# RWKV state chain moved one unit later, its steps interleaved with the next units' matmul groups

## The chip, the core and the metric

One core of one Trainium2 chip runs the whole program. The metric is the device time of one execution in microseconds (us), lower being better. Executions of this kernel are compared by the median of several runs; traces come from one profiled execution.

## What is computed

One decoder layer over a sequence of 1024 tokens of width 1024, in float32. A combined projection feeds three token mixers (RWKV-7, latent attention called MLA, differential attention), their outputs are gated, summed and projected, and a convolutional feed-forward network follows. The change is in the RWKV-7 mixer. It has 8 heads of 64 channels, each with a 64x64 state that every token updates:

```python
def step(state, inp):
    r_t, w_t, k_t, v_t, kk_t, b_t = inp
    sa = jnp.einsum('bhij,bhj->bhi', state, -kk_t)
    state = (state * w_t[:, :, None, :] + sa[..., None] * b_t[:, :, None, :]
             + v_t[..., None] * k_t[:, :, None, :])
    return state, jnp.einsum('bhij,bhj->bhi', state, r_t)
```

The outputs are then normalised per head (`ln_w`, `ln_b`), a bonus term `(sum r*k*r_k) * v` is added, and the result is multiplied by a gate.

## The kernel before, in words

**Units and chunks.** RWKV is cut into 8 units: four pairs of heads `p`, each in two halves `f` of 512 tokens. A unit holds 8 chunks `c` of 64 tokens; the two heads of a pair lie on partitions 0 to 63 and 64 to 127. The work inside a chunk is turned into matrix products, so that only one small matrix recurrence is left from chunk to chunk, the chain of states.

**The three parts of a unit.** `rw_front` (L465) makes the decays and keys: two low-rank products (tile `lps`, two passes each), a norm (`pss`, `prx`), the bonus (`pbo`, L532 to L537), two groups `pA` of products within the chunks, a group of transposes `ptb`, and, by two trips through DRAM (`zf`, `ze`) and 30 short VectorE instructions (`zt`, `zd`, L568), the inverses of 16x16 blocks. `rw_back` (L588) has nine groups of small matmuls, `ptv`, `ph`, `pe`, `ph`, `pe`, `pk`, `pg`, `pq`, `pw`, `pyc`, which leave `ft`, `fc`, `qt`, `yc`. `rw_chain` (L673) runs the chain: for each chunk, two 64x64 matmuls `pr` (L694), and one VectorE instruction that makes the next state `st` (L695); then the group `py`, and the normalisation, two groups of transposes `pty`, the gate product `lpg`, and a store to DRAM (L728). Each of these matmuls is float32 and shows as two passes in the trace, so a chain step is `pr` x4.

**The loop.** `rwkv` (L347) goes over the 8 units: front of unit n, the projections of the next pair in every second iteration (`project`, L350), then back and chain of unit n-1. After the loop come back and chain of the last unit.

**What sets the order.** The program is traced in this order and a scheduler reorders it: each engine takes, of the instructions that its model of the time says are ready, the one with the highest priority, which is the order of tracing; `later` (L366) lowers the priority of projections by 500000, of fills by a million. `keep_in_program_order` pins an instruction behind the one traced before it on its engine. Between fixed points the scheduler is free.

**Fills.** 40 blocks of the combined projection that RWKV doesn't need (tile `gps`, 48 matmuls of 128x512 each, `fills` L385, evicted to `sp` and stored to `pD`) are cover for the waits of RWKV. `nfill` (L67) says how many are traced after each iteration: 3, then 4 seven times, then 3 and 3, 37 in all; the last three are traced after RWKV (L1734). `fill` (L373) paces them: 60% (`share`) of an iteration's fill matmuls are spread evenly over the `mark`s that RWKV set in that iteration, from the fourth mark on (`skip` 3), each not to be issued before its mark; the other 40% come after the last mark. The three last ones have one mark, the last of RWKV. Marks stand before nearly every group of `rw_back` and before each chain step.

**Buffers.** Tiles from `T1` have one buffer: among them `ft`, `fc`, `qt`, `yc`, `kp`, `st`. PSUM has one buffer for each of the tags `ms`, `ab`, `ch`, `y`. Weight loads of fills and projections share two buffers `raw`.

**After RWKV.** `mla_open` (L1234) loads what the MLA mixer needs (`craw`, L931) into memory that RWKV's tiles held and makes keys `kps` and queries `qps`; the attention proper (`S`, `vps`) begins when the last fills are done.

Of the kernel before, what the change touches and what calls it, by code (L numbers as in the profile page):

```python
# [61 lines left out]
class Emit:  # L62
# [6 lines left out]
    def __init__(self, tc, i, o):  # L69
        self.tc, self.nc, self.i, self.o = tc, tc.nc, i, o  # L70
        self.pace, self.marks, self.marking, self.paced = None, [], False, False
        self.pinned = self.strict = False


    def mm(self, out, lhsT, rhs, start=True, stop=True, **k):
        ins = self.nc.tensor.matmul(out, lhsT, rhs, start=start, stop=stop, **k)  # L76
        if self.pinned:
            self.tc.keep_in_program_order(ins)
        if self.pace is not None:
            marks, total, done = self.pace  # L80
            m = len(marks)
            at = lambda d: min(m - 1, int(d * m / total))
            if done == 0 or at(done) != at(done - 1):
                self.tc.add_manual_dep(ins.ins, marks[at(done)], mybir.DependencyInfo(
                    mybir.DependencyClass.NoSync, mybir.DependencyReason.DATA), reason="issue order")
            self.pace[2] += 1
        self.marked(ins)

    def tr(self, out, in_, ident):
        ins = self.nc.tensor.transpose(out, in_, ident)  # L90
        if self.pinned:
            self.tc.keep_in_program_order(ins)
        self.marked(ins)

# [200 lines left out]
    def rwkv(self, rc, r1, r2, zp, pp):  # L295
# [48 lines left out]
        units = [(p, f) for p in range(4) for f in range(2)]  # L344
        state, prev = None, None
# [118 lines left out]

    def rw_front(self, par, p, f, rt, kt, vt):  # L465

# [7 lines left out]

        ps = lora(self.lw[0], self.lx[0], A, p, f)
        th = T1("th")
        self.act(th, ps, AF.Tanh, scale=0.5, bias=self.hw0[:, p:p + 1])
        self.ts(th, th, 1.0, 1.0, ALU.mult, ALU.add, pool)
        cs = T1("cs")
# [19 lines left out]

        ps = lora(self.lw[0], self.lx[0], B, p, f)  # L500
        ta = T1("ta")
        self.act(ta, ps, AF.Tanh, scale=0.5, bias=self.ha0[:, p:p + 1])
        kp = T1("kp")
# [26 lines left out]
        self.tt(bk[:, :, 1], c3(kp), bk[:, :, 1], ALU.mult, pool)  # L530

        self.stt(kp, rt, self.v("rk", p), kp, ALU.mult, ALU.mult)  # L532
        pm = pp.tile([128, 512], F32, tag="ms", name="pbo")
        self.mm(pm, self.bones, kp)
        bv = u["bv"] = T2("bv")
        self.tt(bv, pm, vt, ALU.mult)
        self.ts(bv, bv, 1.0, self.v("lnb", p), ALU.mult, ALU.add, pool)  # L537


        am = u["am"] = T2("am", (128, 2, 8, 3, 64))  # L540
        for q in range(2):
            self.mark()
            pA = pp.tile([128, 2, 4, 2, 64], F32, tag="ab", name="pA")
            for c in range(4):
                for h, hs in half:
                    self.mm(pA[:, h, c].rearrange("p s t -> p (s t)"),
                            bk[hs, 4 * q + c, h:h + 2].rearrange("p s t -> p (s t)"),
                            ar[hs, 4 * q + c, 2:4].rearrange("p s t -> p (s t)"))
            for h, hs in half:
                self.tt(am[:, h, 4 * q:4 * q + 4, 0:2].rearrange("p c s t -> p c (s t)"),  # L550
# [26 lines left out]
        u["ze"] = self.ze[par]  # L577
        return u

# [7 lines left out]

    def rw_back(self, u):  # L588

# [10 lines left out]
        sv = T1("sv", (128, 3, 8, 64))  # L600
        self.mark()
        pt = pp.tile([128, 2, 8, 64], F32, tag="ab", name="ptv")
# [6 lines left out]
        for l in range(2):  # L609
            ml = T1("ml", (128, 8, 64))  # L610
            for h, hs in half:
                self.tt(ml[hs], am[hs, h, :, 0], self.lvl[hs, l].unsqueeze(1).to_broadcast([64, 8, 64]), ALU.mult, pool)
            self.mark()
# [11 lines left out]
            if l == 1:  # L625
                em = T1("ml", (128, 8, 64))
# [7 lines left out]
        self.mark()  # L634
        pk = pp.tile([128, 8, 64], F32, tag="ms", name="pk")
        for c in range(8):
            for h, rs, os in ((0, B, A), (1, A, B)):
                self.mm(pk[os, c], am[rs, h, c, 0], sv[rs, h, c])
        self.act(sv[:, 2], pk)
        self.mark()  # L640
        pg = pp.tile([128, 8, 2, 64], F32, tag="ab", name="pg")
        for c in range(8):
            for h, hs in half:
                self.mm(pg[hs, c], em[hs, c], sv[hs, h:3:2 - h, c])
        gt = T1("hm", (128, 8, 64))
        self.act(gt, pg[:, :, 0])
        for h, hs in half:
            vec.tensor_copy(sv[hs, h], pg[hs, :, 1])
        self.mark()
        pq = pp.tile([128, 8, 2, 64], F32, tag="ab", name="pq")  # L650
        for c in range(8):
            for h, hs in half:
                self.mm(pq[hs, c], gt[hs, c], am[hs, h, c, 1:3])
        qt = u["qt"] = T1("qt", (128, 8, 64))
# [3 lines left out]
        self.mark()  # L658
        pw = pp.tile([128, 8, 64], F32, tag="ms", name="pw")
        for c in range(8):  # L660
            for h, hs in half:
                self.mm(pw[hs, c], am[:, h, c, 2], sv[:, h, c])
        fc = u["fc"] = T1("fc", (128, 8, 64))
        self.tt(fc, pw, gam[:, 1:9].unsqueeze(2).to_broadcast([128, 8, 64]), ALU.mult)
        self.mark()
        pw = pp.tile([128, 8, 64], F32, tag="ms", name="pyc")
        for c in range(8):
            for h, hs in half:
                self.mm(pw[hs, c], am[:, h, c, 1], sv[:, h, c])
        yc = u["yc"] = T1("yc", (128, 8, 64))  # L670
        self.act(yc, pw)

    def rw_chain(self, u, state):  # L673
        nc = self.nc
# [4 lines left out]
        c3 = lambda t: t.rearrange("p (c t) -> p c t", c=8)  # L679
        p, f, gam = u["p"], u["f"], u["gam"]  # L680
        ft, fc, qt = u["ft"], u["fc"], u["qt"]
        st = T1("st", (128, 9, 64))
        if f == 0:
            pool.memset(st[:, 0], 0.0)
        else:
            self.ts(st[:, 0], state, gam[:, 0:1])
        for c in range(8):
            if f == 0 and c == 0:
                vec.tensor_copy(st[:, 1], fc[:, 0])
                continue  # L690
            self.mark()
            pr = pp.tile([128, 64], F32, tag="ch", name="pr")
            for h, hs in half:
                self.mm(pr[hs], ft[hs, c], st[hs, c])  # L694
            self.stt(st[:, c + 1], pr, gam[:, c + 1:c + 2], fc[:, c], ALU.mult, ALU.add)  # L695
        end = T2("end", (128, 64))
        vec.tensor_copy(end, st[:, 8])
        self.mark()
        py = pp.tile([128, 8, 64], F32, tag="y", name="py")
        for c in range(8):  # L700
            for h, hs in half:
                self.mm(py[hs, c], qt[hs, c], st[hs, c])

        y = u["yc"]
        self.tt(y, py, y, ALU.add)
        m8 = T1("m8", (128, 8))
# [21 lines left out]
        nc.sync.dma_start(self.oD[0, p, :, 512 * f:512 * f + 512], ot)  # L728
        return end

# [1113 lines left out]
```

## Time and profile before

| | |
|---|---|
| runs shown, median (lowest to highest) | 2108.87 us (2105.81 to 2109.48), 3 runs |
| the profiled execution | 2112.69 us |
| its span in the trace | 2110.9 us |
| TensorE (PE) busy, weight loads (PEld) busy | 96%, 77% |
| VectorE (DVE), ScalarE (ACT), GpSimd (POOL) busy | 55%, 39%, 34% |

The span is the time from the first to the last instruction of the program; the execution's time has 1.8 us around it. RWKV and its fills take the stretch from about 97 to 893 us. In the rows a matmul's `busy` time includes the drain of the pipeline, so consecutive matmuls overlap in the trace; what a matmul costs is read from start to start. "issue" as the end of an idle time means that the engine waited for nothing that the profile shows.

### The profile page before, as it was taken

What the parts mean: (1) busy time and instruction counts of PE and PEld (TensorE: products, weight loads), DVE (VectorE), ACT (ScalarE), POOL (GpSimd) and SP (SyncE); (2) the same over time, 40 slices, a digit from 0 to 9 for tenths busy, and PEclk for the clock granted to TensorE, in tenths of its full rate; (3) what the DMA queues carried; (4) which work ended last, traced back from release to release, by engine and by line L of the source; (5) the groups of instructions that cost most, each with busy time, mean ns of one, the idle gap of its engine ahead of it and who ended that gap; (6) DMA issues with size and microseconds to landing.
All of it is one profiled execution on the core that took longest, in us unless ns stands there. A gap on an engine that the chain in (4) does not pass through costs nothing. (4 is left out here: it accounts for less than half of the span.)

```text
span 2110.9 us, 32553 instructions
## 1 busy us (share of the span) xinstructions
PE 2034.2 (96%) x12554; PEld 1625.7 (77%) x12554; DVE 1154.0 (55%) x2273; ACT 826.4 (39%) x1449; POOL 709.8 (34%) x577
## 2 busy tenths in 40 slices
PE   7999999999999999999989898999999999999998
PEld 6877777777777777777768776787788888888887
DVE  7135254343534532476777786457866677653534
ACT  5332322232222221577555553234544444442332
POOL 3143243243333322446143656313534433400000
PEclk9999999999999999999989999999999999999999
DMA  5213122212213223320066645353222222264641
GB/s 183 87 62 91 56 73 66 75 66 79 80 46 94 65 66 104 105 65 11 16 211 185 178 135 192 111 181 111 90 90 91 74 77 90 80 238 146 228 141 66
DMA packets 141565, 221.83 MB, mean 105 GB/s; under 512 B 61632, under 2 KB 65600, under 8 KB 141408
## 3 DMA queue, kind: packets, MB, share of 16 engines
q1 hardware_dynamic: 141264, 219.21, 32.0%
q8 instruction: 99, 1.62, 0.3%
q14 instruction: 58, 0.48, 0.1%
q10 hardware_dynamic: 144, 0.52, 0.1%
HBM read 162.53 MB, written 57.16 MB: 104 GB/s over the span
## 5 line engine op out<-in xcount | busy, mean ns | idle before, releaser
L76 PE MATMUL gps<-hhi,whi 128*128 128x512 f32 (+1 forms) x880 | 345.6, 396 | 8.4 <-ACT sp L102 5.9
L76 PE MATMUL gps<-hlo,whi 128*128 128x512 f32 (+1 forms) x880 | 341.6, 391 | 0.0
L109 POOL TENSOR_TENSOR wlo<-wraw,whi 128x512 fp32r<-128x512 f32 x130 | 169.9, 1317 | 297.6 <-PE gps L76 148.7
L76 PE MATMUL gps<-hhi,wlo 128*128 128x512 f32 (+1 forms) x880 | 226.1, 393 | 2.1 <-DVE lx L119 1.7
L76 PEld LDWEIGHTS gps<-hhi,whi 128*128 128x128 f32 x880 | 167.2, 190 | 49.7 <-ACT sp L102 7.5
L76 PEld LDWEIGHTS gps<-hlo,whi 128*128 128x128 f32 x880 | 167.2, 190 | 35.9 <-issue 3.7
L76 PEld LDWEIGHTS gps<-hhi,wlo 128*128 128x128 f32 x880 | 157.4, 188 | 43.1 <-issue 6.8
L109 POOL TENSOR_TENSOR rs_r<-rs_v,phalf 128x1 f32<-128x1 f32 (+2 forms) x43 | 40.5, 942 | 386.0 <-DVE rs_v L116 376.6
L102 ACT ACTIVATE whi<-wraw 128x512 fp32r<-128x512 f32 x130 | 81.4, 628 | 188.0 <-DMA wraw<-in_w_rest_dram 107.2
L102 ACT ACTIVATE L<-L,m 128x128 f32<-128x128 f32 (+7 forms) x128 | 98.9, 773 | 67.6 <-DVE m L109 46.6
L102 ACT ACTIVATE wh<-wsum 128x512 fp32r<-128x512 f32 x109 | 68.5, 630 | 129.5 <-PE ups_b L76 56.0
L109 POOL TENSOR_TENSOR wl<-wraw,wh 128x512 fp32r<-128x512 f32 x43 | 58.3, 1358 | 150.9 <-PE ups_c L76 109.8
L109 DVE TENSOR_TENSOR wsum<-wraw 128x512 f32<-128x512 f32 x110 | 82.0, 749 | 40.6 <-POOL wl L109 39.4
L119 DVE SCALAR_TENSOR_TENSOR st<-pr,gam,fc 128x64 f32<-128x64 f32 x60 | 17.0, 283 | 128.0 <-PE pr L76 127.8
L109 DVE TENSOR_TENSOR gl<-graw,gh 128x512 fp32r<-128x512 f32 x42 | 28.9, 691 | 105.1 <-ACT gh L102 105.1
L90 PE MATMUL ptp<-ident,L 128*128 128x128 f32 x432 | 72.2, 282 | 9.8 <-DVE L L119 2.6
L109 POOL TENSOR_TENSOR wl<-wsum,wh 128x512 fp32r<-128x512 f32 x43 | 57.4, 1336 | 72.0 <-PE ups_b L76 53.8
L102 ACT ACTIVATE gh<-graw 128x512 fp32r<-128x512 f32 x42 | 26.4, 632 | 128.7 <-PE dps__20229 L76 63.6
L90 PEld LDWEIGHTS ptp<-ident,L 128*128 128x128 f32 x432 | 48.9, 141 | 26.3 <-issue 15.0
L902 DVE CUSTOM_DVE_ANT_0 L<-S,mband,rq 128x512 f32<-128x512 f32 (+3 forms) x96 | 57.2, 612 | 18.1 <-PE S L76 9.0
L102 ACT ACTIVATE cvp<-C,cw 128x1024 f32<-128x1024 f32 x44 | 53.1, 1207 | 29.4 <-DVE C L109 19.0
L102 ACT ACTIVATE sp<-gps,hbg 128x512 f32<-128x512 f32 x48 | 33.0, 687 | 75.3 <-PE gps L76 69.8
(769 smaller groups left out, 5119.6 us busy)
## 6 DMA issues: line engine op xcount, KB each, us to landing
wraw<-in_w_up_dram SPq DMA_DIRECT2D x44, 512.0 KB, 4.3
wdr<-in_w_down_dram SPq DMA_DIRECT2D x42, 512.0 KB, 3.4
wraw<-in_w_rest_dram SPq DMA_DIRECT2D x80, 256.0 KB, 2.9
pD<-sp SPq DMA_DIRECT2D x78, 256.0 KB, 2.0
gth<-pD SPq DMA_DIRECT2D x48, 256.0 KB, 2.9
gD<-cv SPq DMA_DIRECT2D x21, 512.0 KB, 2.6
graw<-gD SPq DMA_DIRECT2D x42, 256.0 KB, 2.6
x<-in_x_dram SPq DMA_DIRECT2D x16, 512.0 KB, 6.1
```

What stands on the lines that cost most here:

```text
L76: ins = self.nc.tensor.matmul(out, lhsT, rhs, start=start, stop=stop, **k)
L90: ins = self.nc.tensor.transpose(out, in_, ident)
L102: return self.kept(self.nc.scalar.activation(out, in_, func, **kw))
L109: self.kept((eng or self.nc.vector).tensor_tensor(out, a, b, op))
L119: return self.kept(self.nc.vector.scalar_tensor_tensor(out, a, s, b, op0, op1))
L902: self.nc.vector.tensor_tensor_reduce(L[:, c0:c0 + w], ps[:, :w], bias[:, c0:c0 + w], scale, 3.0e38, ALU.add, ALU.min, acc)
```

## The change

The chain of unit n-2 is now traced during the front of unit n and the back of unit n-1. `chain_steps` is a generator; `step()` takes its next step, right after a group has been traced (both `pA`, `ptb`, first `ph`, `pe` with `pk`, second `ph`, second `pe`, `pg`). `next_on_pe` pins the first matmul that follows it behind the instruction traced before it on TensorE. The same is done for the second low-rank product (`lpa`, right behind `lps`), for `pk` behind `pe`, and for `pw` and `pyc` behind `pq`. What follows the chain is `chain_out`, after the back; the bonus comes after it. Only the last unit's chain is alone (`alone=True`), with marks as before. Chain steps and the pinned groups set no mark otherwise, so that an iteration with front and back has 12 marks. The loop has a ninth iteration without a front, and its fill: 40 fills are traced within RWKV.

```diff
     def mm(self, out, lhsT, rhs, start=True, stop=True, **k):
         ins = self.nc.tensor.matmul(out, lhsT, rhs, start=start, stop=stop, **k)
-        if self.pinned:
+        if self.pinned or self.follow:
             self.tc.keep_in_program_order(ins)
+            self.follow = False
...
-        for n, (p, f) in enumerate(units):
-            u = self.rw_front(n % 2, p, f, *[raw.pop((nm, p, f)) for nm in "rkv"])
+        for n, (p, f) in enumerate(units + [(None, None)]):
+            steps = self.chain_steps(last, state) if last else iter(())
+            step = lambda: next(steps, None)
+            if p is not None:
+                u, bonus = self.rw_front(n % 2, p, f, *[raw.pop((nm, p, f)) for nm in "rkv"], step)
+            if prev:
+                self.rw_back(prev, step)
+            for _ in steps:
+                pass
+            if last:
+                state = self.chain_out(last)
+            if p is not None:
+                bonus()
             if f == 1 and p < 3:
                 with self.later(500000):
                     project(p + 1)
-            if prev:
-                self.rw_back(prev)
-                state = self.rw_chain(prev, state)
-            prev = u
+            prev, last = u, prev
             self.fill(fills, self.nfill[n + 1])
-        self.rw_back(prev)
-        self.rw_chain(prev, state)
+        for _ in self.chain_steps(last, state, True):
+            pass
+        self.chain_out(last)
         self.fill(fills, self.nfill[9])
...
+    def next_on_pe(self):
+
+        self.follow = True
...
         ps = lora(self.lw[0], self.lx[0], A, p, f)
+        self.next_on_pe()
+        psa = lora(self.lw[0], self.lx[0], B, p, f, pp.tile([128, 512], F32, tag="ms", name="lpa"))
...
+            step()
             for h, hs in half:
                 self.tt(am[:, h, 4 * q:4 * q + 4, 0:2].rearrange("p c s t -> p c (s t)"),
...
+        ml = levels(0)
+
         self.mark()
         pt = pp.tile([128, 2, 8, 64], F32, tag="ab", name="ptv")
...
+            self.next_on_pe()
+            pk = pp.tile([128, 8, 64], F32, tag="ms", name="pk")
+            for c in range(8):
+                for h, rs, os in ((0, B, A), (1, A, B)):
+                    self.mm(pk[os, c], am[rs, h, c, 0], sv[rs, h, c])
+            step()
             self.tt(de, pe, de, ALU.add)
...
+        step()
         gt = T1("hm", (128, 8, 64))
         self.act(gt, pg[:, :, 0])
         for h, hs in half:
             vec.tensor_copy(sv[hs, h], pg[hs, :, 1])
+
+        while step():
+            pass
         self.mark()
         pq = pp.tile([128, 8, 2, 64], F32, tag="ab", name="pq")
...
+        self.next_on_pe()
+        pw = pp.tile([128, 8, 64], F32, tag="ms", name="pw")
...
+        self.next_on_pe()
+        py = pp.tile([128, 8, 64], F32, tag="y", name="pyc")
...
+    def chain_steps(self, u, state, alone=False):
...
+        for c in range(1 - u["f"], 8):
+            if alone:
+                self.mark()
+            else:
+                self.next_on_pe()
+            pr = pp.tile([128, 64], F32, tag="ch", name="pr")
             for h, hs in half:
+                self.mm(pr[hs], ft[hs, c], st[hs, c])
+            self.stt(st[:, c + 1], pr, gam[:, c + 1:c + 2], fc[:, c], ALU.mult, ALU.add)
+            if c == 7:
+                self.next_on_pe()
+                py = u["py"] = pp.tile([128, 8, 64], F32, tag="y", name="py")
+                for k in range(8):
+                    for h, hs in half:
+                        self.mm(py[hs, k], qt[hs, k], st[hs, k])
+                end = u["end"] = self.T2("end", (128, 64))
+                vec.tensor_copy(end, st[:, 8])
+                y = u["y"] = st[:, 0:8]
+                self.tt(y, py, u["yc"], ALU.add)
+            yield True
```

## Rows read from the trace of the kernel before

**Rows 1.** The page: span, then busy time, share and instructions of each engine.

```profile
span 2110.9 us, 32553 instructions
PE 2034.2 (96%) x12554; PEld 1625.7 (77%) x12554; DVE 1154.0 (55%) x2273; ACT 826.4 (39%) x1449; POOL 709.8 (34%) x577
```

**Rows 2.** Windows: busy us (and instructions) by engine, granted clock, DMA share, GB/s.

```profile
97.00:615.00 518.00, 511.37 (x4001) 394.06 (x4000) 215.97 (x522) 140.19 (x242) 178.65 (x158) 0.99 0.23 68
```

**Rows 3.** Timeline of PE: start, us, engine, line, operation, tiles, count. A lone chain step.

```profile
430.60 0.39 PE L76 MATMUL gps<-hhi,whi 128*128 128x512 f32 x1
430.82 0.39 PE L76 MATMUL gps<-hlo,whi 128*128 128x512 f32 x1
431.14 0.33 PE L76 MATMUL pr<-st,ft 64*64 64x64 f32 x4
...
431.52 0.50 PE L76 MATMUL gps<-hhi,whi 128*128 128x512 f32 x1
431.86 0.39 PE L76 MATMUL gps<-hlo,whi 128*128 128x512 f32 x1
```

**Rows 4.** Timeline of PE, a chain step behind another group, and `py` alone before it.

```profile
405.65 0.33 PE L76 MATMUL py<-st,qt 64*64 64x64 f32 x4
...
405.91 1.15 PE L76 MATMUL pyc<-sv,am 128*64 128x64 f32 x32
...
406.99 0.33 PE L76 MATMUL pr<-st,ft 64*64 64x64 f32 x4
...
407.15 0.28 PE L76 MATMUL py<-st,qt 64*64 64x64 f32 x4
...
407.37 0.53 PEld L76 LDWEIGHTS gps<-hhi,wlo 128*128 128x128 f32 x3
```

**Rows 5.** Tile `pr`: what its engine waited for (us, times).

```profile
  issue: 12.3, 36
```

**Rows 6.** Groups of PE and PEld, 97 to 893 us: count | busy, mean ns | idle before.

```profile
L76 PEld LDWEIGHTS gps<-hlo,whi 128*128 128x128 f32 x767 | 145.2, 189 | 33.1 <-issue 3.7
L76 PE MATMUL pq<-am,hm 64*64 64x128 f32 x256 | 15.7, 272 | 1.9 <-DVE sv L648 1.9
L76 PEld LDWEIGHTS pr<-st,ft 64*64 64x64 f32 x240 | 12.0, 131 | 16.8 <-issue 12.3 <-DVE st L119 2.3 <-DVE sq L517 1.1
```

**Rows 7.** Timeline: the end of a unit's projections, where the weights change.

```profile
414.53 0.33 PE L76 MATMUL pr<-st,ft 64*64 64x64 f32 x4
...
415.25 0.33 PE L76 MATMUL pr<-st,ft 64*64 64x64 f32 x4 [0.27 <-DVE st L119]
...
416.38 0.47 PE L76 MATMUL gps<-hhi,whi 128*128 128x512 f32 x1 [0.69 <-DVE kt L119]
```

**Rows 8.** Groups of POOL and DVE, 97 to 893 us, columns as in rows 6.

```profile
L109 POOL TENSOR_TENSOR ml<-am,lvl 64x512 f32<-64x512 f32 x32 | 41.5, 1296 | 33.1 <-PE ph L76 18.6 <-PE pg L76 13.3
L109 DVE TENSOR_TENSOR zd<-zd,zt 64x15 f32<-64x15 f32 (+7 forms) x120 | 40.1, 334 | 3.8
L119 DVE SCALAR_TENSOR_TENSOR st<-pr,gam,fc 128x64 f32<-128x64 f32 x60 | 17.0, 283 | 128.0 <-PE pr L76 127.8
L116 POOL TENSOR_SCALAR kp<-ta,hka,cka 128x512 f32<-128x512 f32 x8 | 6.7, 836 | 2.5 <-PE pbo L76 2.4
```

**Rows 9.** Tile `ot`: the store of a unit on the SP queue (ns minimum, median, maximum).

```profile
L728 SPq DMA_DIRECT2D oD<-ot x8: 326/332/1468, 293.3 to 836.6; - x8
```

**Rows 10.** Timeline, end of RWKV to the end of the last query.

```profile
846.30 0.63 ACT L102 ACTIVATE whi<-wraw 128x512 fp32r<-128x512 f32 x1 [6.60 <-DMA wraw<-in_w_rest_dram]
...
850.59 0.80 PE L76 MATMUL gps<-hhi,whi 128*128 128x512 f32 x1 [5.09 <-ACT sp L102]
...
885.45 0.68 DVE L109 TENSOR_TENSOR qtl<-qf,qth 32x512 fp32r<-32x512 f32 x1 [0.80 <-ACT qth L102]
```

**Rows 11.** Windows after that stall, columns as in rows 2.

```profile
851.00:860.00 9.00, 9.00 (x30) 7.10 (x30) 7.23 (x8) 3.76 (x9) 2.98 (x4) 0.72 0.55 173
```

**Rows 12.** End of RWKV, window 835 to 893 us of tile `gps` (columns as rows 2, without POOL).

```profile
835.00:893.00 58.00, 46.52 (x186) 36.65 (x186) 0.00 (x0) 5.48 (x8) 0.94 0.43 129
```

More of the change, by code (lines that the diff above doesn't have):

```diff
@@ L76, in mm @@
         ins = self.nc.tensor.matmul(out, lhsT, rhs, start=start, stop=stop, **k)
-        if self.pinned:
+        if self.pinned or self.follow:
             self.tc.keep_in_program_order(ins)
+            self.follow = False
         if self.pace is not None:
@@ L90, in tr @@
         ins = self.nc.tensor.transpose(out, in_, ident)
-        if self.pinned:
+        if self.pinned or self.follow:
             self.tc.keep_in_program_order(ins)
+            self.follow = False
         self.marked(ins)
@@ L344, in rwkv @@
         units = [(p, f) for p in range(4) for f in range(2)]
-        state, prev = None, None
+        state, prev, last = None, None, None
         project(0)
-        for n, (p, f) in enumerate(units):
-            u = self.rw_front(n % 2, p, f, *[raw.pop((nm, p, f)) for nm in "rkv"])
+        for n, (p, f) in enumerate(units + [(None, None)]):
[11 more added lines that the diff above has]
+                bonus()
             if f == 1 and p < 3:
@@ L463, in lora, with rw_front @@
         return ps
-    def rw_front(self, par, p, f, rt, kt, vt):
+    def rw_front(self, par, p, f, rt, kt, vt, step):
         nc = self.nc
@@ L530, in rw_front, with bonus @@
         self.tt(bk[:, :, 1], c3(kp), bk[:, :, 1], ALU.mult, pool)
[L532 to L537, printed above, removed]
+        def bonus():
+            self.stt(kp, rt, self.v("rk", p), kp, ALU.mult, ALU.mult)
+            pm = pp.tile([128, 512], F32, tag="ms", name="pbo")
+            self.mm(pm, self.bones, kp)
+            bv = u["bv"] = T2("bv")
+            self.tt(bv, pm, vt, ALU.mult)
+            self.ts(bv, bv, 1.0, self.v("lnb", p), ALU.mult, ALU.add, pool)
         am = u["am"] = T2("am", (128, 2, 8, 3, 64))
@@ L577, in rw_front @@
         u["ze"] = self.ze[par]
-        return u
+        return u, bonus
     @staticmethod
@@ L586, in diag, with rw_back @@
         return bass.AP(t.tensor, t.offset + 66560 * m, [[1040, 64], [64, 16], [1, 16]])
-    def rw_back(self, u):
+    def rw_back(self, u, step):
         nc = self.nc
@@ L600, in rw_back, with levels @@
         sv = T1("sv", (128, 3, 8, 64))
+        def levels(l):
+            ml = T1("ml", (128, 8, 64))
+            for h, hs in half:
+                self.tt(ml[hs], am[hs, h, :, 0], self.lvl[hs, l].unsqueeze(1).to_broadcast([64, 8, 64]), ALU.mult, pool)
+            return ml
+        ml = levels(0)
         self.mark()
@@ L609, in rw_back @@
         for l in range(2):
[L610 to L613, printed above, removed]
+            if l:
+                ml = levels(1)
+                self.mark()
             ph = pp.tile([128, 8, 64], F32, tag="ms", name="ph")
@@ L625, in rw_back @@
             if l == 1:
+                step()
                 em = T1("ml", (128, 8, 64))
@@ L631, in rw_back @@
                     self.mm(pe[hs, 0, c], em[hs, c], hm[hs, c])
-            self.tt(de, pe, de, ALU.add)
[L634 to L639, printed above, removed]
+            self.next_on_pe()
[3 more added lines that the diff above has]
+                    self.mm(pk[os, c], am[rs, h, c, 0], sv[rs, h, c])
+            step()
+            self.tt(de, pe, de, ALU.add)
+            self.act(sv[:, 2], pk)
         self.mark()
@@ L644, in rw_back @@
                 self.mm(pg[hs, c], em[hs, c], sv[hs, h:3:2 - h, c])
+        step()
         gt = T1("hm", (128, 8, 64))
@@ L653, in rw_back @@
                 self.mm(pq[hs, c], gt[hs, c], am[hs, h, c, 1:3])
+        self.next_on_pe()
+        pw = pp.tile([128, 8, 64], F32, tag="ms", name="pw")
+        for c in range(8):
+            for h, hs in half:
+                self.mm(pw[hs, c], am[:, h, c, 2], sv[:, h, c])
+        self.next_on_pe()
+        py = pp.tile([128, 8, 64], F32, tag="y", name="pyc")
+        for c in range(8):
+            for h, hs in half:
+                self.mm(py[hs, c], am[:, h, c, 1], sv[:, h, c])
         qt = u["qt"] = T1("qt", (128, 8, 64))
@@ L657, in rw_back, with chain_out @@
         self.tt(ft, pq[:, :, 1], self.id64.unsqueeze(1).to_broadcast([128, 8, 64]), ALU.add)
[L658 to L662, printed above, removed]
         fc = u["fc"] = T1("fc", (128, 8, 64))
         self.tt(fc, pw, gam[:, 1:9].unsqueeze(2).to_broadcast([128, 8, 64]), ALU.mult)
-        self.mark()
-        pw = pp.tile([128, 8, 64], F32, tag="ms", name="pyc")
-        for c in range(8):
-            for h, hs in half:
[L669 to L673, printed above, removed]
+        yc = u["yc"] = T1("yc", (128, 8, 64))
+        self.act(yc, py)
+    def chain_steps(self, u, state, alone=False):
+        nc = self.nc
+        pool, vec, pp = nc.gpsimd, nc.vector, self.pp
+        half = ((0, slice(0, 64)), (1, slice(64, 128)))
+        ft, fc, qt, gam = u["ft"], u["fc"], u["qt"], u["gam"]
+        st = u["st"] = self.T1("st", (128, 9, 64))
+        if u["f"] == 0:
+            pool.memset(st[:, 0], 0.0)
+            vec.tensor_copy(st[:, 1], fc[:, 0])
+        else:
+            self.ts(st[:, 0], state, gam[:, 0:1])
+        for c in range(1 - u["f"], 8):
+            if alone:
+                self.mark()
+            else:
+                self.next_on_pe()
+            pr = pp.tile([128, 64], F32, tag="ch", name="pr")
+            for h, hs in half:
+                self.mm(pr[hs], ft[hs, c], st[hs, c])
[4 more added lines that the diff above has]
+                for k in range(8):
+                    for h, hs in half:
+                        self.mm(py[hs, k], qt[hs, k], st[hs, k])
[4 more added lines that the diff above has]
+            yield True
+    def chain_out(self, u):
         nc = self.nc
@@ L679, in rw_chain @@
         c3 = lambda t: t.rearrange("p (c t) -> p c t", c=8)
[L680 to L705, printed above, removed]
+        p, f, y = u["p"], u["f"], u["y"]
         m8 = T1("m8", (128, 8))
@@ L728, in rw_chain @@
         nc.sync.dma_start(self.oD[0, p, :, 512 * f:512 * f + 512], ot)
-        return end
+        return u["end"]
     def bias_band(self, sp, pp):
```

5 lines of the change are left out of this document (2 added, 3 removed).

## The prediction

> **What bounds the kernel now.** I read the page first: PE is busy 96% of the span, the other engines at most 55% [rows 1]. A busy share says little of a pipelined engine, so I looked at the stretch that the change touches. From 97 to 615 us PE is busy 511 of 518 us, at a granted clock of 0.99 [rows 2]. Hardly anything there waits: fills stand in every hole. So a shorter latency of the chain buys nothing by itself; PE's own sequence has to get shorter. What can get shorter is seen in the timeline. Fills follow each other by 0.22 to 0.23 us (430.60 to 430.82; 0.23 below). A lone chain step with its share of `py` takes 1.04 us from the last fill before it to the second after it, where two fill steps take 0.46: it costs **0.58** [rows 3]. The same pair behind `pyc` costs 0.38 (406.99 to 407.37) [rows 4]. The difference, 0.20, is what entering and leaving a run of small matmuls costs: the first comes 0.32 after the last fill instead of 0.23, and the first fill after the run takes 0.50 instead of 0.39 [rows 3]. The tile view of `pr` counts the entries that waited for nothing but "issue": 36 [rows 5], of 60 steps (240 loads, four a step) [rows 6].
>
> **The change, part by part.**
>
> *Steps behind groups.* 36 lone steps lose 0.20 each: 36 x 0.20 = **-7.2 us**. The steps that today join another run by chance gain nothing. At least none lands well (0), at most all 60 count (-12); I take the 36 counted.
>
> *`py` in one group.* In a step `py` costs 0.38 - 0.26 = 0.12, since four passes of this shape alone take 0.26 (`py` at 405.65, `pyc` at 405.91) [rows 4]. So 60 x 0.12 + 4 x 0.26 (units with f = 0 have a `py` without `pr`) = 8.2 now. Eight groups of 32 passes at 1.08, by `pyc` of the same size (405.91 to 406.99) [rows 4], are 8.6: **+0.4**.
>
> *Pinned pairs.* `lpa` behind `lps` and `pyc` behind `pw` save a run each per unit: 2 x 8 x 0.20 = **-3.2**; some already share a run, so 0 is the other end. `pk` mostly follows `pe` already: 0. `pq` waited 1.9 us in all for `sv` [rows 6]; nothing makes those copies earlier, so 0 of a possible -1.9.
>
> *What chain steps covered.* While projection weights change, two steps stand in the hole, and PE still waits 0.69 (414.53 to 416.38) [rows 7]. Without them the hole opens by up to 2 x 0.38 = 0.76. Three pairs are projected: 0 to +2.3, I take half, **+1.1**.
>
> *What moves with the chain.* The 60 `st` instructions of 0.283 us run a unit later, among the fronts' DVE work; a step's successor comes a whole group later, and a `zd` or `zt` ahead of it takes 0.334 [rows 8]: 0. If the scheduler queued one behind the whole string of 30, a step would hold PE's queue for up to 10 us; that I only count as a bound. The bonus is traced after `chain_out`; POOL's `kp` of the next front waits for `pbo` already today, 2.5 us [rows 8]; POOL is 34% busy [rows 1] and DVE has room, so 0, bounded by that wait again, +2.5. The first `ml` moves ahead of `ptv`: two of 1.3 us on POOL [rows 8], in front of a split of weights whose fill is double-buffered: 0 to +1. The store of a unit moves on SP behind the next back's loads, 0.33 us of issue [rows 9], with weight loads behind it, again double-buffered: 0. Normalisation and `pty` move with it, unchanged.
>
> *Fewer marks, and all fills inside.* Marks per iteration fall from about 25 to 12, so a fill waits for coarser points; cover is the 40% that no mark holds: 0 in the middle. At the end it matters, see the second rival.
>
> Sum: -7.2 + 0.4 - 3.2 + 1.1 = **-8.9 us**. The profiled execution took 2112.69 us, 3.8 above the median of the runs shown; the sum against it gives 2103.8, and against the median 2108.87 - 8.9 = **2100.0 us**. A measurement of this kernel can tell about 0.2%, 4.2 us, from no change. With 20 to 48 lone steps saved, half or all of the pairs and 0 to 2.3 for the hole, this case reaches from 2096 to 2105.
>
> **The rivals.**
>
> *1. The stall at the end goes as well.* Before 850.59 us PE waits 5.09 us: ScalarE stood for 6.60 at a fill's weights that were late [rows 10]; afterwards the granted clock is 0.72 for 9 us, in which 30 matmuls go that take 6.9 at full speed [rows 11], 2.1 lost. With fills used up earlier their weights need not come in then. That gives 7.2 more: 2092.8. For: all fills are now paced inside RWKV. Against: something must cover the opening of MLA. Chance 0.12.
>
> *2. The end lies bare, slower.* Today 186 fill matmuls remain after RWKV [rows 12]: the three fills behind its last mark, and most of the 58 matmuls (40% of three fills) that no mark holds. They cover the opening of MLA, which runs from about 835 to 886.1 (`qtl`) [rows 10], 44.5 without the 6.6 that ScalarE stood. With 40 fills paced inside, only the 58 are sure to be left: 58 x 0.23 = 13.3, and the 30 matmuls of the first keys and queries 6.9. So PE idles 44.5 - 20.2 = 24.3 us, where it loses 7.2 today: +17.1, and with the sum +8.2: **2117.1**. It decides from the number left at the last gate product: below about 97 (where idle time, 44.5 - 6.9 - 0.23 x 97, is 7.2 + 8.9) the kernel gets slower. For: fills slip into every hole where marks allow them, so they will be eaten. Against: a shorter sequence of stages per unit lets RWKV end earlier, with more left. Chance 0.22.
>
> *3. The steps don't land behind their groups.* A pin says "after", not "right after". If the scheduler's model sees a state ready later than the group ends, fills slip in and the 0.20 stays; only the pairs remain: -8.9 + 7.2 = -1.7, 2107.2. For: there is no other constraint. Against: a state has the time of a whole group, and stepping through DVE takes 0.72 (414.53 to 415.25) [rows 7]. Chance 0.20.
>
> *4. Runs cost more at their ends than one place shows.* If the loads at both ends lay bare, 0.131 for a step's and 0.189 for a fill's [rows 6], a run would cost 0.32 and not 0.20, and 52 runs fewer would bring 6.2 more: 2093.8. The trace speaks against it: fills have loads of 0.189 and still start every 0.23 [rows 3, 6], and the places read give 0.20. Chance 0.06. The Trainium skill, "TensorE: Matmul & The Clock Gate", Part 3 (The mechanism), says that a weight load overlaps matmuls in flight only when its row group differs; by that rule the ends, where 128 rows meet 64, lie bare as here, and the sum would be this rival's. Fills, which use the same 128 rows one after another, do not obey it in this trace.
>
> **How the numbers follow.** The forecast itself has 0.40. Nearly all of it, with rivals 1 and 4, is faster by over 0.2%: 0.56. Rival 3, the forecast's slow edge and the mild part of rival 2 are within 0.2%: 0.24. The rest of rival 2 is slower: 0.20. The range leaves out the fastest corner of rivals 1 and 4 and the worst half of rival 2: 2091 to 2115.
>
> **What would show it.** In the changed kernel's tile view `pr` should have few waits for "issue", about 10 instead of 36, and in the timeline `pr` x4 should stand directly behind `pA`, `ptb`, `ph`, `pk`, `pe` or `pg`. `py` should be x32. `lpa` should follow `lps` without a fill between. PE's window from 97 us to the first `S` should be shorter by some 9 us. Rival 1 shows as no wait near the end; rival 2 as well under 100 `gps` after the last `lpg` and PE idle before `kps` and `qps`; rival 3 as `gps` rows between group and `pr`. I am wrong at the root if PE's start-to-start cost inside a run turns out larger than 0.26 per step, or if PE waits for `st` at pinned steps.

## The result, and the profile after

The changed kernel takes 2120.25 us (median of 5 runs, 2116.48 to 2129.89), the kernel before 2108.87 in the same comparison: ratio **1.0055, 95% interval 1.0035 to 1.0075**. It is slower; the prediction, 2100.0 with a range to 2115, was wrong. The profiled execution took 2126.92 us.

First the page, and the window and the tile view that answer to [rows 1], [rows 2] and [rows 5].

```profile
span 2124.8 us, 32557 instructions
PE 2026.2 (95%) x12554; PEld 1637.9 (77%) x12554; DVE 1141.3 (54%) x2273; ACT 828.7 (39%) x1449; POOL 713.3 (34%) x577
```

```profile
97.00:615.00 518.00, 510.61 (x4029) 406.06 (x4029) 205.06 (x523) 146.55 (x253) 188.16 (x167) 0.99 0.24 72
```

```profile
its engine sat idle before it (us, times) until:
...
  issue: 2.8, 8
  DVE st L122: 2.7, 6
```

The page tells nothing: PE did the same 12554 matmuls in 8 us less busy time, in a span 13.9 longer. The tile view of `pr` says that the change did what it set out to do: 8 lone entries for "issue" where there were 36. The timeline of PE (start, duration, count) shows what a step then costs, where [rows 3] and [rows 4] showed 0.58 and 0.38.

```profile
383.68 0.39 PE L77 MATMUL gps<-hhi,whi 128*128 128x512 f32 x1
384.00 1.15 PE L77 MATMUL ph<-de,ml 64*64 64x64 f32 x32
384.98 0.28 PE L77 MATMUL pr<-st,ft 64*64 64x64 f32 x4
385.19 0.50 PE L77 MATMUL gps<-hlo,whi 128*128 128x512 f32 x1
...
393.38 1.96 PE L77 MATMUL pg<-sv,ml 64*64 64x128 f32 x32
395.18 0.28 PE L77 MATMUL pr<-st,ft 64*64 64x64 f32 x4
395.30 1.10 PE L77 MATMUL py<-st,qt 64*64 64x64 f32 x32
396.32 0.50 PE L77 MATMUL gps<-hhi,wlo 128*128 128x512 f32 x1
```

Inside a run four passes of `pr` cost **0.12** (395.18 to 395.30). `ph` with a step lasts 1.19 from its start to the fill behind it (384.00 to 385.19); `ph` alone, which stands in both kernels, 1.08.

The loss lies around the end of RWKV. These windows (PE, PEld, DVE, ACT, POOL busy, granted clock) end at the last gate product `lpg`, near the first `S`, and at the last `O`, with which MLA ends; first the kernel before, then the changed one.

```profile
97.00:835.00 738.00, 729.18 (x5964) 560.30 (x5963) 303.90 (x728) 193.61 (x329) 253.99 (x221) 1.00 0.23 70
835.00:894.00 59.00, 53.91 (x223) 43.35 (x222) 24.78 (x32) 28.96 (x44) 24.10 (x21) 0.94 0.42 127
894.00:1071.00 177.00, 175.32 (x1308) 135.40 (x1307) 120.56 (x339) 116.54 (x259) 70.97 (x59) 1.00 0.13 37
```

```profile
97.00:850.00 753.00, 733.00 (x6085) 582.32 (x6085) 288.50 (x727) 200.78 (x341) 260.34 (x226) 0.99 0.25 74
850.00:883.00 33.00, 25.03 (x96) 19.58 (x94) 22.95 (x28) 20.09 (x29) 15.03 (x15) 0.87 0.57 148
883.00:1078.00 195.00, 186.06 (x1320) 143.15 (x1318) 126.90 (x344) 120.17 (x264) 74.18 (x62) 0.94 0.08 24
```

PE idles 20.0 us instead of 8.8 in the first window (its length less PE's busy time), then 8.0 instead of 5.1, then 8.9 instead of 1.7, and from 850 on at a lower clock. The tile `gps` behind the last `lpg`, which answers to [rows 12] (186 there), PE's waits from 850 on (us in total, times, longest), and the clock of the stretch behind them, answering to [rows 11]:

```profile
850.00:867.00 17.00, 15.64 (x67) 12.63 (x68) 0.00 (x0) 2.02 (x3) 1.00 0.47 136
```

```profile
PE S L77 <- ACT qth L105: 5.2, 2, 2.8
PE qps L77 <- DVE lamv L112: 4.6, 1, 4.6
PE qps L77 <- DVE kt1l L122: 3.3, 1, 3.3
PE qps L77 <- DVE qtl L112: 2.4, 1, 2.4
```

```profile
878.00:898.00 20.00, 12.54 (x36) 9.95 (x37) 14.86 (x30) 11.16 (x26) 10.77 (x8) 0.50 0.37 92
```

**68 fill matmuls are left, and the last one starts at 867.2 us** (just behind the window, whose line has 67 of them), when VectorE and ScalarE are still busy opening MLA. `qps` waits for them three times, between 867.6 and 885.9 us, `S` twice, from 889 and from 946 us. From 878 us on PE stands at 0.50, the lower of its two levels, for 20 us: a pass of `qps` there follows the one before it by 0.43 us (880.68 to 881.11) instead of 0.23 (874.41 to 874.64). The stall of [rows 10] is gone: no wait of 5 us for `sp`. A bare end stands in its place.

### The profile page after: what moved, and what is told of

Its sections match the earlier page's. It is cut to its first block, busy times and chain, and to the rows that moved or that the text cites. A ratio compares the mean times of both kernels' runs of the same rounds, so it can differ in the third digit from the quotient of the medians.

```text
span 2124.8 us, 32557 instructions
## 1 busy us (share of the span) xinstructions
PE 2026.2 (95%) x12554; PEld 1637.9 (77%) x12554; DVE 1141.3 (54%) x2273; ACT 828.7 (39%) x1449; POOL 713.3 (34%) x577
## 5 line engine op out<-in xcount | busy, mean ns | idle before, releaser
L77 PE MATMUL gps<-hhi,wlo 128*128 128x512 f32 (+1 forms) x880 | 221.4, 391 | 2.8 <-DVE lx L122 1.7
```

## The account that the experiments are read by

For each trace, from 97 us to the last `lpg`, I count the fill and projection matmuls (`gps`, with 16 small ones that are the same in every kernel) at 0.2265 us each (the 0.22 to 0.23 of [rows 3]), PE's idle time, and what the lower clock cost (half of PE's busy time at 0.50, an estimate from the 0.43 against 0.23 above). What is left I call RWKV's own work on PE. Each kernel was profiled twice (experiment 5): 236.1 and 236.3 before, 208.4 and 208.5 changed, so the account holds to a few tenths. "Holes" are idle time and the cost of the lower clock together.

| kernel | ratio to before (95%) | last `lpg` at | `gps` until then, after it | idle | clock | own work | last `O` at |
|---|---|---|---|---|---|---|---|
| before | 1 | 835.1 | 2163, 186 | 8.8 | 3.4 | 236 | 1071.1 |
| changed | 1.0055 (1.0035 to 1.0075) | 850.1 | 2285, 68 | 20.0 | 7.2 | 208 | 1077.7 |
| three left | 0.9951 (0.9937 to 0.9966) | 833.1 | 2168, 186 | 25.9 | 11.5 | 208 | 1061.9 |
| before, 40 inside | 1.0115 (1.0098 to 1.0132) | 862.1 | 2302, 42 | 7.0 | 1.7 | 235 | 1092.5 |
| three left, no pins | 1.0068 (1.0053 to 1.0083) | 853.8 | 2174, 186 | 24.3 | 13.4 | 227 | 1081.6 |
| steps pinned alone | 0.9969 (0.9953 to 0.9985) | 835.1 | 2170, 186 | 22.4 | 9.5 | 215 | 1062.9 |
| pairs pinned alone | 1.0043 (1.0028 to 1.0057) | 848.3 | 2170, 186 | 27.9 | 10.1 | 222 | 1076.1 |
| `pr` twice | 0.9955 (0.9940 to 0.9970) | 830.9 | 2160, 186 | 22.9 | 6.9 | 215 | 1059.3 |
| levels back | 1.0030 (1.0019 to 1.0041) | 848.2 | 2171, 186 | 34.7 | 20.1 | 205 | 1076.2 |
| marks at steps | 1.0043 (1.0026 to 1.0059) | 851.9 | 2175, 180 | 36.3 | 16.9 | 209 | 1080.0 |
| skip 0 | 0.9970 (0.9956 to 0.9984) | 826.1 | 2166, 185 | 22.9 | 5.0 | 211 | 1056.4 |

So the change takes 28 us off RWKV's own work. Of these, 15 go to more idle time (+11.2) and the lower clock (+3.8) in the middle. At the end, from the last `lpg` to the last `O`, it saves only 8.4 us (236.0 to 227.6) though 118 fill matmuls (26.7) have gone from there: 18.3 lost. The 18.3 are about what idle time (16.9 instead of 6.8) and the lower clock (11.4 instead of 2.8) cost more there. With four fill matmuls more done ahead than are missed behind (+1.0): -27.7 + 15.0 + 1.0 + 18.3 = +6.6, the difference at the last `O`.

## The experiments

**1. The end.** Two edits separate the three fills from all the rest. In the changed kernel:

```diff
-            self.fill(fills, self.nfill[n + 1])
+            if p is not None:
+                self.fill(fills, self.nfill[n + 1])
```

> The changed kernel, but its ninth iteration traces no fills: 37 blocks are paced within RWKV and three are left behind its last mark, as before the change. Theory A (the end lies bare: the changed kernel left 68 fill matmuls behind the last lpg where 186 stood before, and the rest of RWKV got shorter): some 190 matmuls after the last lpg, no idle PE before the first S beyond 10 us, half clock there under 10 us, and 2090 to 2103 us, faster than both. Theory B (the slowdown comes from PE waiting at pinned steps and groups in the middle; the end is only shifted): the waits of the middle stay and the time stays between 2112 and 2122.

And in the kernel before:

```diff
-    nfill = [3, 4, 4, 4, 4, 4, 4, 4, 3, 3]
+    nfill = [3, 4, 4, 4, 4, 4, 4, 4, 6, 3]
```

> The kernel before, with six instead of three blocks traced after the eighth unit's front, so that all 40 are paced within RWKV; the chain stays where it was. Theory A: RWKV ends later with 60 to 100 fill matmuls left, the MLA opening lies bare, and the kernel gets slower by 8 to 17 us: 2117 to 2126. Theory B: the number left does not matter, 2105 to 2112.

Measured: 2102.63 us (ratio 0.9951) and 2134.65 (1.0115). The windows of PE from the last `lpg` to the first `S`, all work, first with three left, then the kernel before with 40 inside, and the two largest waits of PE in the latter up to 960 us:

```profile
833.00:885.00 52.00, 51.57 (x224) 41.63 (x223) 24.96 (x32) 29.05 (x45) 24.97 (x21) 1.00 0.39 119
```

```profile
862.00:898.00 36.00, 20.28 (x70) 14.62 (x69) 23.99 (x28) 21.47 (x29) 15.27 (x13) 0.79 0.73 203
```

```profile
PE qps L76 <- DVE qtl L109: 9.5, 2, 8.2
PE qps L76 <- DVE kt1l L119: 6.5, 2, 6.3
```

With three left PE is busy 51.57 of 52 us at full clock. Without them it stands 15.7 of 36 us in the old kernel (8.0 of 33 in the changed one), and the old kernel came out slower than the 2117 to 2126 us expected, with 42 fill matmuls left and not 60 to 100. The bare end is the cause of the slowdown: the same three fills turn a gain of 10 us into a loss of 11, and cost the old kernel 24. That is more than idle time: from the last `lpg` to the last `O` the old kernel lost 17.8 us more by it and 8.9 more by the lower clock. Moved inside RWKV, the three fills of the changed kernel close 10.2 us of holes there (25.9 and 11.5 fall to 20.0 and 7.2 in the table); behind the last `lpg` 118 fill matmuls, 26.7 us, are gone, and yet the stretch is only 1.2 us shorter (228.8 to 227.6).

**2. How many to leave.** Two left (one fill paced in the ninth iteration, 2108.77 us, ratio 0.9982, 0.9970 to 0.9994), four left (`nfill[9]` is 2 instead of 3, 2101.30, 0.9959, 0.9943 to 0.9974), and three left with one fill of the eighth iteration moved into the ninth (2105.53, 0.9971, 0.9959 to 0.9982). Against the kernel with three left, the edits are, in this order:

```diff
-            if p is not None:
-                self.fill(fills, self.nfill[n + 1])
+            self.fill(fills, self.nfill[n + 1] if p is not None else 1)
```

```diff
-    nfill = [3, 4, 4, 4, 4, 4, 4, 4, 3, 3]
+    nfill = [3, 4, 4, 4, 4, 4, 4, 4, 3, 2]
```

```diff
-    nfill = [3, 4, 4, 4, 4, 4, 4, 4, 3, 3]
+    nfill = [3, 4, 4, 4, 4, 4, 4, 4, 2, 3]
...
-            if p is not None:
-                self.fill(fills, self.nfill[n + 1])
+            self.fill(fills, self.nfill[n + 1] if p is not None else 1)
```

> The changed kernel, but the ninth iteration paces one fill instead of three: 38 fills within RWKV, two left. Theory A (what counts is whether the fills left after the last gate product still cover the opening of MLA): the number left falls to some 120 to 150, between the 68 of the changed kernel and the 186 with three left, so PE stays nearly unbroken before the first S (under 3 us idle), and the one fill fills part of the 10 us that PE stands at the last two transposes pty: 2098 to 2103 us. Rival (each fill moved in front of the last gate product costs its own length, whatever is left): a third of the way from 2102.6 to 2120, 2107 to 2110 us.

> The changed kernel with four fills left after RWKV, 36 paced within it. Theory A (the opening of MLA is already covered with three left; a fourth only delays the first S, and the last iterations lose cover): RWKV ends 5 to 10 us earlier, about 230 fill matmuls come after the last gate product, the first S stays where it was or is up to 5 us later: 2102 to 2107 us. Rival (more cover at the end always pays, the optimum lies further on): below 2100 us.

> The changed kernel with three fills left, but one of the fills of the eighth iteration is paced in the ninth, so that the last unit is not without cover. In the kernel with three left PE stands 10.2 us at two transposes pty of the last iteration. Theory E (these holes are open because no fill is left to be issued there, and earlier iterations have enough): 5 to 8 us of them are filled, 2094 to 2098 us, still 186 fill matmuls after the last gate product. Rival (fills are the same in number wherever they stand, so the hole only opens an iteration earlier): 2101 to 2104 us.

With four left the time stands, as the theory had it (209 matmuls behind the last `lpg`, where some 230 were expected; last `O` at 1063.8). With two left, 164 remained, not 120 to 150; the last `O` came at 1063.5, only 1.6 later than with three, but the kernel took 6.5 us longer (0.0031 of the ratio). Its number fits the rival (each fill moved costs its own length), its trace up to the last `O` does not. Moving a fill left 212 matmuls behind the last `lpg`, not 186, and brought the last `O` forward by 4.8 us, to 1057.1; the kernel took 4 us longer all the same (0.0020 of the ratio), which neither side expected. Idle time before the last `lpg` stayed at 26.6. In both the stretch behind the last `O` was longer, with more time at the lower clock in it (30.7 and 23.9 us, against 13.7). Why is open; see experiment 5.

**3. What the pins are worth, and what a step costs.** In the kernel with three left, `next_on_pe` does nothing; then it is left out at `lpa`, `pk`, `pw`, `pyc`; then at `pr` and `py` alone; then each `pr` is issued twice. In this order:

```diff
     def next_on_pe(self):
...
-        self.follow = True
+        self.follow = False
```

```diff
-        self.next_on_pe()
         psa = lora(
...
-            self.next_on_pe()
             pk = pp.tile(
...
-        self.next_on_pe()
         pw = pp.tile(
...
-        self.next_on_pe()
         py = pp.tile([128, 8, 64], F32, tag="y", name="pyc")
```

```diff
-            else:
-                self.next_on_pe()
             pr = pp.tile(
...
-                self.next_on_pe()
                 py = u["py"] = pp.tile(
```

```diff
             for h, hs in half:
                 self.mm(pr[hs], ft[hs, c], st[hs, c])
+            for h, hs in half:
+                self.mm(pr[hs], ft[hs, c], st[hs, c])
```

> The first of these three kernels without any pin: steps, lpa, pk, pw and pyc are traced in the same place, but the scheduler may put them anywhere. If the pins make the steps cheap (they keep them inside runs), the number of small runs rises by 20 or more and the time by 3 to 10 us against the first. If the order of tracing does it alone, or the pins cost waits as theory B has it, the time is the same or lower.

> The changed kernel with three fills left, but lpa, pk, pw and pyc are not pinned; only the chain steps (pr) and py are. The pins together were worth 22 us. Theory B (nearly all of it is the chain steps that land inside a run, and py in one group): the four pairs give away some 0.4 us a unit at pw and pyc and 0.2 at lpa: 2104 to 2108 us. Rival (the pairs carry as much as the steps, or the gain needs the whole order to be fixed): 2112 us or more.

> The changed kernel with three fills left, but pr and py are not pinned; lpa, pk, pw and pyc still are. Theory B (chain steps carry the gain): 2116 to 2122 us, with pr x4 py x4 again as runs of their own between fills. Rival (pairs carry half): 2108 to 2113 us.

> The changed kernel with three fills left, and every chain step's two matmuls pr issued twice into the same tile, so that a step is eight passes. It measures what a step costs inside a run. Theory D (a step behind a group of 64x64 costs 0.12 us, not the 0.26 that the prediction took from the place behind pyc): a run of ph and a step, 1.195 us with one step, takes 1.31, and the time rises by 60 x 0.12 = 7 us, to about 2110, if the scheduler keeps its order. Rival (0.26 a step, as predicted): 1.45 us for that run, and 2118 us.

Without pins the kernel takes 2125.15 us, 22.5 more, where 3 to 10 were expected: own work 227 instead of 208. With the steps pinned alone it takes 2104.35 (own work +7: the pairs' worth), with the pairs alone 2120.36 (+14: the steps' worth); together they are about the 19. So a pin is not idle advice: without it fills slip between group and step, as rival 3 feared. The tile view of `pr` without pins:

```profile
  issue: 15.2, 37
```

Without pins own work is still 9 us below the 236 of the kernel before; that part belongs to the new order of tracing, and no experiment divides it further. With `pr` twice, the run of `ph` and a step reads:

```profile
382.40 1.15 PE L77 MATMUL ph<-de,ml 64*64 64x64 f32 x32
383.38 0.40 PE L77 MATMUL pr<-st,ft 64*64 64x64 f32 x8
383.71 0.50 PE L77 MATMUL gps<-hhi,whi 128*128 128x512 f32 x1
```

1.31 (382.40 to 383.71) against 1.19, so 0.12 a step, and own work rises by 7.2 us, which is 60 x 0.12. The time did not rise to the 2110 that were expected if the order stayed (2101.19): the holes fell by 7.6 in the new order. An edit of 7 us can thus vanish in the holes.

**4. Whence the holes in the middle.** PE's waits in the changed kernel, up to the last `lpg` at 850 us, the five largest (us in total, times, longest); the kernel before, below, has only one of over 2 us:

```profile
PE pty L92 <- POOL st L112: 4.2, 2, 3.7
PE pe L77 <- DVE sv L634: 3.5, 3, 2.1
PE ptv L92 <- ACT am L105: 2.6, 2, 1.6
PE gps L77 <- DVE kt L122: 1.8, 3, 0.6
PE pA L77 <- DVE am L112: 1.2, 1, 1.2
```

```profile
PE ph L76 <- DMA de<-ze: 2.5, 1, 2.5
```

At the worst of `pe`, 553.64 us, VectorE's copy `sv` had its input, the transposes `ptv`, at 550.42, and started at 552.38, behind `zt` and `zd` in its queue (timeline, PE and DVE):

```profile
549.71 0.71 PE L92 MATMUL ptv<-ident,ar 64*128 64x64 f32 x16
...
552.24 0.21 DVE L112 TENSOR_TENSOR zd<-zd,zt 64x60 f32<-64x60 f32 x1
552.38 1.21 DVE L634 COPY sv<-ptv 128x1024 f32<-128x1024 f32 x1
...
553.64 1.12 PE L77 MATMUL pe<-de,hm 64*64 64x64 f32 x16 [2.07 <-DVE sv L634]
```

In the kernel with three left two waits of PE at `pty`, near the end of RWKV, make 10.2 of the 25.9 us of idle time; with one fill moved into the last iteration (experiment 2) they still make 8.1.

Three edits of the kernel with three left: `levels(0)` called after `ptv` again, with a mark before the first `ph`; a mark again at every step and before `pk`, `pw`, `pyc`; `skip` 0 instead of 3.

```diff
-        ml = levels(0)
...
-            if l:
-                ml = levels(1)
-                self.mark()
+            ml = levels(l)
+            self.mark()
```

```diff
+            self.mark()
             self.next_on_pe()
             pk = pp.tile(
...
+        self.mark()
         self.next_on_pe()
         pw = pp.tile(
...
+        self.mark()
         self.next_on_pe()
         py = pp.tile([128, 8, 64], F32, tag="y", name="pyc")
...
-            if alone:
-                self.mark()
-            else:
+            self.mark()
+            if not alone:
                 self.next_on_pe()
```

```diff
-    share, skip = 0.6, 3
+    share, skip = 0.6, 0
```

> The changed kernel with three fills left, and the first ml made where it was before, after ptv. PE idles 26 us between 97 us and the last gate product where the kernel before idles 9; this asks what opened those holes. Theory C (not this: the holes come from the order that the scheduler chose by its model, with VectorE's strings of zt and zd ahead of the copy sv, and from the last iteration, which has no fill to cover pty): idle within 3 us of 26, time within 3 us of 2102.6. Rival (the early ml takes POOL's time before the weights of fills): idle falls by 5 us or more, 2094 to 2099 us.

> The changed kernel with three fills left, and a mark again at each chain step and before pk, pw and pyc, as many as the kernel before has; the pins stay. Theory C (the holes are waits at the head of PE's queue that no mark could fill): idle 23 to 29 us, time 2100 to 2106 us. Rival (coarse marks keep fills from the holes, as the prediction priced at 0): idle falls by 8 us or more and with it the stretches at the half clock, 2090 to 2096 us.

> The changed kernel with three fills left, and fills allowed from the first mark of an iteration on instead of the fourth. Theory C: the order moves a little, idle stays above 20 us, 2100 to 2106 us. Rival (fills are held back just where pA, ptb and ptv wait): the waits before pA, ptb and ptv go, 5 us with their half clock, 2094 to 2098 us.

Measured: 2117.15, 2120.04 and 2103.88 us. `skip` 0 brought the last `O` forward by 5.5 us, with 9.5 us less in holes up to the last `lpg`, but the time did not fall. The other two made it worse, by 14.5 and 17.4 us, which neither side expected; idle time rose to 35 and 36 us. The two largest waits of the first:

```profile
PE pty L92 <- POOL st L112: 10.4, 2, 5.9
PE pA L77 <- DVE am L112: 8.9, 3, 4.2
```

There `pA` follows a step with no fill between, and waits for VectorE to empty its PSUM buffer:

```profile
642.21 0.33 PE L77 MATMUL pr<-st,ft 64*64 64x64 f32 x4
646.69 1.22 PE L77 MATMUL pA<-ar,bk 64*128 64x128 f32 x8 [4.15 <-DVE am L112]
```

So PE waits at the head of its own queue, with no fill in it ahead of `pA`. That the scheduler's model expects VectorE and ScalarE earlier than they come is what I infer from this; the model itself stands in no trace. Which groups end up side by side hangs on small edits. That marks as such are harmful is not shown; the same edit moves the order too. With `levels(0)` back own work fell by 3 us and the holes grew by 17: the loss came by the order that resulted, and whether the late `ml` or its mark brought that order about is not separated.

**5. What came after MLA.** Of the 13.9 us between the first two profiles, 7.1 arose after the last `O`, in code that the change leaves alone. Both kernels were profiled again, unedited.

> The changed kernel as it is, profiled a second time. In the first profile, 6.7 us above the median of its runs, the stretch from the last O (the end of MLA) to the last matmul took 1039.5 us, where the kernel before took 1032.4, with 37.5 us at the half clock against 20.5, in code that the change doesn't touch. Theory F (a matter of the one execution: holes of a few us fall differently against the clock each time): 1030 to 1036 us this time. Rival (it belongs to this kernel's order of work): 1038 to 1041 us again.

> The kernel before as it is, profiled a second time, as the other half of that comparison: from the last O to the last matmul 1032.4 us in the first profile. Theory F: anywhere from 1029 to 1040 us, not tied to the 1032.4. Rival: 1031 to 1034 us again.

From the last `O` to the last matmul it took 1033.4 us (changed) and 1031.7 (before) this time, against 1039.5 and 1032.4. The windows of the changed kernel, first and second profile:

```profile
1078.00:2117.00 1039.00, 999.20 (x4603) 823.85 (x4602) 655.42 (x1045) 442.99 (x736) 338.95 (x245) 0.98 0.41 136
```

```profile
1075.00:2109.00 1034.00, 993.49 (x4610) 819.37 (x4605) 656.09 (x1046) 441.81 (x737) 337.72 (x245) 0.99 0.41 136
```

The granted clock was 0.98 and 0.99. For the changed kernel 6 of the 7.1 us belonged to the one execution, while everything up to the last `O` came out alike: idle 20.0, 8.0 and 8.9 us in both profiles. The 1031.7 of the kernel before fits both sides of its expectation. In all sixteen profiles this stretch took 1028.6 to 1039.8 us, though no edit touches its code. Whether the kernels with two left and with one fill moved owe their time there to the kernel or to chance is not shown; their medians of 10 runs speak for the kernel. So the account stops at the last `O`: it explains 6.6 us (5 in the second pair of profiles) of the 11.4 between the medians of the two kernels, and the rest stays open.

## Why the prediction was wrong

- **Which case.** What happened is the second rival, which had 0.22. It stood at 2117.1, with some 58 fill matmuls left and 24.3 us idle; there were 68, 16.9 us of idle time from the last `lpg` to the last `O` (6.8 before), and 11.4 us lost at the lower clock on top (2.8 before), which it had left out. The step of the forecast that failed is "Fewer marks, and all fills inside": its sum has nothing for the end, which lost 18.3 us. I held against the rival that a shorter sequence of stages leaves more. But the 186 of [rows 12] are 3 x 48 = 144 of the three fills behind the last mark, and 42 others. The change moves the 144 inside, so 42 were to be expected (the old kernel with 40 inside left exactly 42; the shorter sequence gave 26 more), and the rival's own threshold was 97. The rows decided it, and I weighed it as a possibility.
- **Steps behind groups, -6.8 with `py`.** Right in kind, half the size: pinning them is worth 14 us (experiment 3). The price inside a run was read at `pyc`, a group of 128-row tiles: four passes of `py` ahead of it take 0.26. Behind a 64x64 group four passes take 0.12. With a step's share of `py` at 0.14 (eight groups of 1.02, 395.30 to 396.32, over 60 steps), step and share cost 0.26 instead of 0.58 or 0.38, and 36 x (0.58 - 0.26) + 24 x (0.38 - 0.26) = 14.4. That is an estimate, close to the 14 of the pins; what of the 9 us of the new order without pins is the steps' is not known.
- **Pinned pairs, -3.2.** Worth 7. Only in four of eight units does `lpa` stand beside `lps`; in three it comes some 80 us later, since a pin says "after" and not "right after". But where it does, it is nearly free (below).
- **What moves with the chain, and the marks, both 0 in the middle.** Here stand the holes: +11.2 us idle and +3.8 for the clock. It is not `pr` that waits for `st` (1.2 us in all); `pe` waits for `sv`, which did stand behind part of the string of 30, `pty` for POOL, `ptv` and `pA` for the copies that empty their buffers. Marks put back did not close them (experiment 4); which edit opened them is not shown.
- **Rival 1.** Its stall goes, but not for its reason: with three left the stretch from the last `lpg` to the last `O` falls from 236.0 to 228.8, though as many fills are left as before. That this is just the 7.2 it named is luck: the stall was 5.1 us in the first profile of the kernel before and 2.8 in the second, and the stretch 236.0 and 232.7.
- **Rival 3.** Wrong because of the pins. **Rival 4** also: runs of small matmuls fell only from 163 to 130, and a run's ends cost no more than in [rows 3] (0.32 to its start, 383.68 to 384.00, and a fill of 0.50 behind it); the work inside costs less.
- **The sign to look for.** The window to the first `S` did get shorter, by 11.5 us (894.3 to 882.8). It was a bad sign to choose: without fills `S` starts early and then waits.
- **The size.** With three left the ratio is 0.9951, near the -8.9 of the forecast. That is luck: own work fell by 28 us, where its parts on PE's work give 10.0, and 25 went into holes, where the forecast had 1.1; 7.2 came back at the end.
- **Two figures of the prediction.** By its own terms the slow edge of its case is 2106, not 2105 (20 steps, half of the pairs, 2.3 for the hole). The rival's threshold of 97 goes with 0.22 a fill matmul; with the 0.23 used beside it, it is 93. Neither changes the outcome.

## What to carry to other kernels

Count what covers a latency after the change, from the counts of before, and if that falls below what the latency needs, make it the forecast and not a rival. Take the price of moved work from the place where it will stand, behind a neighbour of the same shape. Where a scheduler's model sets the order of an engine's queue, small edits shift holes worth 15 us and more, so judge an edit by the work it takes off and by the holes apart. Here the change with three fills left for the end is 0.5% faster than the kernel before.

## What the hardware showed unexpectedly

Two low-rank products on different halves of the rows run at the same time. Timeline of PE, changed kernel, then `lps` alone in the kernel before:

```profile
425.63 0.69 PE L77 MATMUL lps<-lx,w2a 64*128 64x512 f32 x1
425.64 0.69 PE L77 MATMUL lpa<-lx,w2a 64*128 64x512 f32 x1
426.17 0.59 PE L77 MATMUL lps<-lx,w2a 64*128 64x512 f32 x1
426.18 0.59 PE L77 MATMUL lpa<-lx,w2a 64*128 64x512 f32 x1
426.69 0.73 PE L77 MATMUL gps<-hhi,wlo 128*128 128x512 f32 x2
```

```profile
446.40 1.12 PE L76 MATMUL lps<-lx,w2a 64*128 64x512 f32 x2
447.45 0.73 PE L76 MATMUL gps<-hhi,wlo 128*128 128x512 f32 x2
```

Four passes take 1.06 us (425.63 to 426.69), two alone 1.05. The estimate from this is 1.05 in each of four units, 4.2 of the pairs' 7 us; with the steps pinned alone the two products stand apart in every unit. The Trainium skill, "TensorE: Matmul & The Clock Gate", Part 3 (The mechanism), says that matmuls in different row groups overlap; this trace agrees, and the prediction should have drawn on it here.

In the kernel with three left PE stood 2.43 us before `pe` at 555.20 us, the place of the hole in experiment 4. The windows around it, with the granted clock behind POOL's busy time:

```profile
540.00:553.90 13.90, 12.78 (x92) 9.62 (x88) 6.51 (x26) 3.58 (x6) 1.29 (x1) 1.00 0.31 82
553.90:560.70 6.80, 5.50 (x101) 5.33 (x102) 5.23 (x17) 1.15 (x2) 0.00 (x0) 0.50 0.01 2
```

The two holes at `pty`, 4.5 and 5.6 us long, had such a stretch too, and so had some shorter ones. Up to the last `lpg` these stretches cost 11.5 us beside 25.9 of idle time. A hole's price can be more than its length.
